# A two-layer encoder kernel: convolution sums moved into PSUM, fewer taps on GpSimd, softmax scaling on ScalarE

## The chip, the cores and the metric

The kernel runs on one core of one Trainium2 chip. The metric is the device time of one execution in microseconds (us), as the median of several runs. In the rows, PE is TensorE's matmuls and PEld its weight loads, DVE is VectorE, ACT is ScalarE, POOL is GpSimd, SP is SyncE. A row that begins with ACTq is ScalarE's instruction queue while it issues a DMA.

## What is computed

Two layers of an encoder run over two sequences of 256 tokens, with 1024 features. Layer 0 mixes with neighbourhood attention and a spatial gate; layer 1, the "second mixer", with latent attention beside a gated convolution of 31 taps. Each layer then has a feed-forward block. All arithmetic is in fp32, and matmuls with weights run on values split into a high and a low part. The change touches these parts of layer 1 (and, by a flag, the helper that both attentions share):

```python
def odd_mixer(x, ...):                      # the second mixer
    h = x @ w_in                            # c_q, c_kv, k_r, glu_a, glu_g
    c = latent_attention(c_q, c_kv, k_r, ...)         # rms norms, 8 heads, softmax
    d = glu_a * jax.nn.sigmoid(glu_g)                 # 512 channels
    d = jax.nn.silu(layernorm(dwconv(d, conv_w, conv_b), conv_ln_g, conv_ln_b))
    return jnp.concatenate([c, d], axis=-1) @ w_out
...
        p = jax.nn.softmax(s, axis=-1).astype(v.dtype)
        return jnp.einsum('bhqk,bkhd->bqhd', p, v_r)
```

`dwconv` is a depthwise convolution: each of the 512 channels is summed over 31 shifted copies of itself, each with its own weight.

## The kernel before

The program is one stream of work written in Python. A scheduler orders each engine's queue from it before the kernel runs; on the chip each engine works its queue strictly in order and waits on semaphores. Pools of tiles decide further waits: PSUM has eight banks of 128x512 fp32, four in pool `pA`, two in `pB`, two in `pC`.

The second mixer goes like this. `glu(i)` makes a quarter of the convolution's input, 128 channels by two sequences of 256 tokens: two groups of 24 matmuls, a sigmoid on ScalarE (`sig`), and a product on VectorE into `dpad[i]`, which has 15 zeros on both sides of each sequence. `cproj()` makes the inputs of the latent attention, and `chain()` norms them: ScalarE copies them from PSUM to `craw` and sums their squares, VectorE and GpSimd make the scale (`v`), VectorE applies it (`craw`, line 585), TensorE transposes. `kvproj()` and `qproj()` make keys, values and queries; the queries' rotary parts go into place by DMAs that ScalarE issues (line 623). `attend(p)` runs for four pairs of heads, each over two sequences, so 16 times in all for one head: scores (`s`) by TensorE into `pB`, the row maximum (`nmx`) on VectorE, the exponential (`er`) with row sums on ScalarE, the reciprocal (`ri`) and the scaling of the rows by it on VectorE (lines 484 to 487), a transpose (`pt`) on TensorE, a copy (`PTr`) on ScalarE, and the product with the values (`pv`).

The convolution has no need of TensorE. For each of the four quarters, VectorE makes the first tap and the bias (line 530) and adds one shifted, weighted copy after the other into `acc` in SBUF (line 680). The last `NPOOL` taps go another way: ScalarE multiplies the shifted input by its weight into a ring of two halves called `pr` (line 684; the first of them, line 532, goes straight into `acc2`), and GpSimd adds it to `acc2` (line 685). Line 686 adds the two sums. The scheduler spreads these instructions over VectorE's, ScalarE's and GpSimd's queues between those of the norms and the attention. After them come a layer norm over the channels (`conv_ln`: transposes `ct` and `cb`), the output projection (`op` and `dn`) and the feed-forward block.

Of the kernel before, what the change touches and what calls it, by code (L numbers as in the profile page):

```python
# [11 lines left out]
AF = mybir.ActivationFunctionType  # L12
# [10 lines left out]
LN_EPS = 1e-5  # L23
RMS_EPS = 1e-6
NPAIR = 22
NPOOL = 13
NWARM = 18
ACUT = 832
KEEP = {4: 0, 7: 1, 10: 2, 13: 3}
# [21 lines left out]
def tile_encoder(ctx: ExitStack, tc: tile.TileContext, I, O):  # L51
    nc = tc.nc
# [411 lines left out]

    pend = []

    def attention(p, score, V, mix, post, er, PTr):
        for s in range(2):
            PT = [PTr.get(), PTr.get()]
            pss = [bank(pB, "s").rearrange("p (a k) -> p a k", a=2) for _ in range(2)]  # L470
            for qt in range(2):
                for h in range(2):
                    score(pss[h][:, qt, :], h, slice(s * S + qt * P, s * S + qt * P + P), slice(s * S, s * S + S))
            for h in range(2):
                e = er.get()
                sc = post(pss[h], h, e)
                nmx = small(2, "nmx")
                nc.vector.tensor_reduce(out=nmx, in_=sc, axis=AX.X, op=ALU.max, negate=True)
                rs = small(2, "rs")
                for qt in range(2):  # L480
                    nc.scalar.activation(out=e[:, qt, :], in_=sc[:, qt, :], func=AF.Exp,  # L481
                                         bias=nmx[:, qt:qt + 1], accum_out=rs[:, qt:qt + 1])
                ri = small(2, "ri")
                nc.vector.reciprocal(out=ri, in_=rs)
                for qt in range(2):
                    nc.vector.tensor_scalar(out=e[:, qt, :], in0=e[:, qt, :], scalar1=ri[:, qt:qt + 1], scalar2=None,  # L486
                                            op0=ALU.mult)
                pt = bank(pC, "pt")
                for kc in range(2):
                    for qt in range(2):  # L490
                        nc.tensor.transpose(pt[:, (2 * kc + qt) * P:(2 * kc + qt + 1) * P],  # L491
                                            e[:, qt, kc * P:(kc + 1) * P], ident)
                nc.scalar.copy(out=PT[h], in_=pt.rearrange("p (k q) -> p k q", k=2))

            def pv_stage(s=s, PT=PT):
                pv = bank(pC, "pv")
                for kc in range(2):
                    for h in range(2):
                        mm(pv[h * 64:(h + 1) * 64, :S], V[s][:, kc, (2 * p + h) * 64:(2 * p + h + 1) * 64],
                           PT[h][:, kc, :], kc == 0, kc == 1)  # L500
                split(mix, pv[:, :S], slice(s * S, s * S + S))
            flush_pv()
            pend.append(pv_stage)
# [9 lines left out]

    def odd_mixer(xT):
        dpad = [None] * 4

        def glu(i, by_seq=False):
            pss = []
            for hi, lo in kept.pop(i, None) or glu_load(i):
                pss.append((bank(pA, "glu"), hi, lo))  # L520
            for seqs in ((0,), (1,)) if by_seq else ((0, 1),):
                for ps, hi, lo in pss:
                    gemm_feat(ps, hi, lo, xT, seqs)
            sg = tmp([P, 512], s="sig")
            nc.scalar.activation(out=sg, in_=pss[1][0], func=AF.Sigmoid)
            d = dpad[i]
            nc.vector.tensor_tensor(out=d[:, :, 15:15 + S], in0=pss[0][0].rearrange("p (s t) -> p s t", s=2),
                                    in1=sg.rearrange("p (s t) -> p s t", s=2), op=ALU.mult)
            a, a2 = acc[i // 2][:, i % 2], acc2[i // 2][:, i % 2]
            nc.vector.tensor_scalar(out=a, in0=d[:, :, 0:S], scalar1=pc("cw", i * 32),  # L530
                                    scalar2=pc("cw", i * 32 + 31), op0=ALU.mult, op1=ALU.add)
            nc.scalar.activation(out=a2, in_=d[:, :, 31 - NPOOL:31 - NPOOL + S], func=AF.Copy,
                                 scale=pc("cw", i * 32 + 31 - NPOOL))

# [116 lines left out]
        def attend(p):  # L651
            if p == 0:
                G["ring"] = Ring(2, "er"), Ring(2, "PTr")
            er, PTr = G["ring"]
            qT, kT = G["qT"], G["kT"]
            mixT[p] = act([P, 2, T], F32R, "mixT")
            if p == 2:
                G["sink"] = ToFeat(xscr[1], 1, last_mm[0], "ln1_g1", "ln1_b1", xscr[2], EARLY)
            attention(p, lambda out, h, qs, ks: mm(out, qT[p][0:96, h, qs], kT[p][0:96, h, ks], True, True),
                      G["V"], mixT[p], lambda ps, h, e: ps, er, PTr)  # L660

        mixT = [None] * 8
        glu(0, True)
# [11 lines left out]
        op = OutProj("wout1", mixT, [0, 1, 2, 3], [4, 5, 6, 7])  # L675
        op.first(0, (0, 1))
        for i in range(4):
            a, a2 = acc[i // 2][:, i % 2], acc2[i // 2][:, i % 2]
            for j in range(1, 31 - NPOOL):
                nc.vector.scalar_tensor_tensor(out=a, in0=dpad[i][:, :, j:j + S], scalar=pc("cw", i * 32 + j), in1=a,  # L680
                                               op0=ALU.mult, op1=ALU.add)
            for j in range(32 - NPOOL, 31):
                pr = pr_ring.get()
                nc.scalar.activation(out=pr, in_=dpad[i][:, :, j:j + S], func=AF.Copy, scale=pc("cw", i * 32 + j))  # L684
                nc.gpsimd.tensor_tensor(out=a2, in0=a2, in1=pr, op=ALU.add)  # L685
            nc.vector.tensor_tensor(out=a, in0=a, in1=a2, op=ALU.add)

        def conv_ln():
            for c in range(4):
# [191 lines left out]
```

## Time and profile before

| | before |
|---|---|
| time, median of 3 runs | 1159.08 us (1159.08 to 1159.62) |
| profiled execution, span | 1159.0 us |
| mean granted TensorE clock | 0.978 of full speed |
| busy share of the span | PE 96%, DVE 61%, ACT 42%, POOL 22% |

The profiled execution's span agrees with the median of the runs within 0.1 us, so a sum made against the span can be read as a time. In the profile, a line that gives 40 digits shows the busy share of 40 equal slices (29 us each) in tenths.

### The profile page before, as it was taken

How to read it: one execution, taken by the hardware profiler on the slowest of the kernel's cores; microseconds unless marked ns; L12 is line 12 of the kernel's file. 1: busy time of each engine (PE TensorE's matmuls, PEld its weight loads, DVE VectorE, ACT ScalarE, POOL GpSimd, SP SyncE). 2: the span in 40 equal slices, each digit the busy share in tenths (PEclk: the TensorE clock that was granted, in tenths of full speed). 3: DMA queues.
4: the chain of work that ended last, by engine and by line, in shares of the span. 5: the costliest groups of instructions: out<-in, count | busy, mean ns of one | idle time of the engine just before them, and what ended most of it. 6: DMA issues, size and time to landing. Idle time of an engine off the chain costs nothing.

```text
span 1159.0 us, 13693 instructions
## 1 busy us (share of the span) xinstructions
PE 1107.0 (96%) x5210; PEld 908.1 (78%) x5210; DVE 702.3 (61%) x1016; ACT 486.3 (42%) x765; POOL 259.1 (22%) x243
## 2 busy tenths in 40 slices
PE   9999999999999999999998658899999999999996
PEld 7787777988888888888887535689888888888884
DVE  3567774775565566323678999657755665642226
ACT  3534552644444444311555467346444444432110
POOL 4091011300000000007376656702000000000174
PEclk9999999999999999999998878999999999999998
DMA  8742104333223224553221121134332232223501
GB/s 254 238 118 73 55 20 171 133 115 108 91 93 108 91 92 140 186 198 100 106 81 49 28 73 43 67 109 140 116 106 95 91 104 97 91 99 101 199 38 73
DMA packets 36194, 124.34 MB, mean 107 GB/s; under 512 B 4352, under 2 KB 5120, under 8 KB 36128
## 3 DMA queue, kind: packets, MB, share of 16 engines
q1 hardware_dynamic: 28224, 99.10, 26.7%
q0 software_dynamic: 6480, 22.66, 5.4%
q10 hardware_dynamic: 1424, 1.71, 0.6%
q8 instruction: 41, 0.67, 0.2%
q14 instruction: 25, 0.20, 0.1%
HBM read 114.01 MB, written 8.39 MB: 106 GB/s over the span
## 4 chain that ended last, share of the span: by engine, by line
PE 83%; DVE 11%; DMA 2%; ACT 1%; issue 1%; POOL 1%; SPq 0%; POOLq 0%; ACTq 0%; DVEq 0%
PE up L96 42%; PE dn L96 25%; DVE acc L680 5%; PE qk L96 4%; PE op L96 4%; DMA raw<-in_wug 2%; PE s L96 2%; PE v L96 2%; DVE er L486 2%; PE pv L96 1%; DVE wlo L109 1%; PE glu L96 1%; PE lnT L233 1%; PE pt L491 1%; PE u L96 1%
## 5 line engine op out<-in xcount | busy, mean ns | idle before, releaser
L96 PE MATMUL up<-xT,whi 128*128 128x512 f32 (+1 forms) x1536 | 440.7, 372 | 0.4 <-DVE xT L245 0.4
L109 DVE TENSOR_TENSOR wlo<-raw,whi 128x1024 fp32r<-128x1024 f32 (+1 forms) x174 | 225.2, 1295 | 303.6 <-ACT whi L107 299.9
L96 PEld LDWEIGHTS up<-xT,whi 128*128 128x128 f32 x1536 | 280.1, 188 | 50.3 <-DVE xT L245 0.6
L107 ACT CAST whi<-raw 128x1024 fp32r<-128x1024 f32 (+1 forms) x174 | 182.5, 1050 | 262.4 <-PE dn L96 126.1
L96 PE MATMUL up<-xT,wlo 128*128 128x512 f32 (+1 forms) x768 | 283.8, 372 | 0.0
L96 PE MATMUL dn<-whi,gT 128*128 128x512 f32 x704 | 217.7, 390 | 0.0
L96 PEld LDWEIGHTS up<-xT,wlo 128*128 128x128 f32 x768 | 144.4, 188 | 25.1
L96 PEld LDWEIGHTS dn<-whi,gT 128*128 128x128 f32 x704 | 132.1, 188 | 27.2
L96 PE MATMUL dn<-wlo,gT 128*128 128x512 f32 x352 | 137.0, 389 | 0.0
L182 POOL DMA_DIRECT2D xres<-xscr x12 | 6.4, 540 | 574.4 <-PE dn L96 573.5
L685 POOL TENSOR_TENSOR acc<-acc,pr 128x512 f32<-128x512 f32 x48 | 77.3, 1610 | 46.4 <-ACT pr L684 44.2
L680 DVE SCALAR_TENSOR_TENSOR acc<-dpad,par,acc 128x512 f32<-128x512 f32 x68 | 78.3, 1177 | 0.5
L96 PEld LDWEIGHTS dn<-wlo,gT 128*128 128x128 f32 x352 | 66.1, 188 | 13.6
L113 ACT CAST gT<-cv 128x512 fp32r<-128x512 f32 x44 | 27.3, 620 | 112.2 <-DVE cv L742 112.2
L731 ACT ACTIVATE cv<-up,par 128x512 f32<-128x512 f32 x88 | 67.9, 772 | 0.0
L734 DVE SCALAR_TENSOR_TENSOR cv<-up,par,cv 128x510 f32<-128x510 f32 x88 | 65.8, 747 | 2.7
L732 DVE SCALAR_TENSOR_TENSOR cv<-up,par,cv 128x510 f32<-128x510 f32 x88 | 65.4, 743 | 0.0
L741 ACT ACTIVATE cv<-cv 128x512 f32<-128x512 f32 x44 | 27.8, 632 | 80.6 <-DVE cv L734 80.6
L114 DVE TENSOR_TENSOR gT<-cv,gT 128x512 fp32r<-128x512 f32 x44 | 30.4, 692 | 27.5 <-ACT gT L113 27.5
L96 PE MATMUL glu<-xT,khi 128*128 128x512 f32 (+1 forms) x160 | 44.0, 362 | 0.0
L96 PE MATMUL op<-whi,mixT 128*128 128x512 f32 x128 | 43.5, 398 | 0.0
L96 PE MATMUL dn<-whi,mixT 128*128 128x512 f32 x128 | 42.6, 395 | 0.7 <-ACT er L481 0.7
(193 smaller groups left out, 1397.8 us busy)
## 6 DMA issues: line engine op xcount, KB each, us to landing
raw<-in_wup SPq DMA_DIRECT2D x88, 512.0 KB, 3.4
raw<-in_wdn SPq DMA_DIRECT2D x44, 512.0 KB, 3.5
raw<-in_wout SPq DMA_DIRECT2D x16, 512.0 KB, 3.7
xscr<-xres POOLq DMA_DIRECT2D x12, 512.0 KB, 3.4
xres<-xscr POOLq DMA_DIRECT2D x12, 512.0 KB, 4.5
raw<-in_wqk SPq DMA_DIRECT2D x8, 512.0 KB, 4.6
raw<-in_wglu SPq DMA_DIRECT2D x8, 512.0 KB, 4.0
raw<-in_wug SPq DMA_DIRECT2D x7, 512.0 KB, 6.6
```

What stands on the lines that cost most here:

```text
L96: last_mm[0] = nc.tensor.matmul(out=out, lhsT=lhsT, rhs=rhs, start=first, stop=last)
L107: nc.scalar.copy(out=hi[:, :n], in_=raw[:, :n])
L109: nc.vector.tensor_tensor(out=lo[:, :n], in0=raw[:, :n], in1=hi[:, :n].bitcast(F32), op=ALU.subtract)
L113: nc.scalar.copy(out=dst[:, 0, sl], in_=src)
L114: nc.vector.tensor_tensor(out=dst[:, 1, sl], in0=src, in1=dst[:, 0, sl].bitcast(F32), op=ALU.subtract)
L486: nc.vector.tensor_scalar(out=e[:, qt, :], in0=e[:, qt, :], scalar1=ri[:, qt:qt + 1], scalar2=None, op0=ALU.mult)
L680: nc.vector.scalar_tensor_tensor(out=a, in0=dpad[i][:, :, j:j + S], scalar=pc("cw", i * 32 + j), in1=a, op0=ALU.mult, op1=ALU.add)
L685: nc.gpsimd.tensor_tensor(out=a2, in0=a2, in1=pr, op=ALU.add)
L731: nc.scalar.activation(out=c, in_=pv, func=AF.Identity, scale=pc(fw, ch * 4 + 1), bias=pc(fw, ch * 4 + 3))
L732: nc.vector.scalar_tensor_tensor(out=c[:, :, 1:S], in0=pv[:, :, 0:S - 1], scalar=pc(fw, ch * 4), in1=c[:, :, 1:S], op0=ALU.mult, op1=ALU.add)
L734: nc.vector.scalar_tensor_tensor(out=c[:, :, 0:S - 1], in0=pv[:, :, 1:S], scalar=pc(fw, ch * 4 + 2), in1=c[:, :, 0:S - 1], op0=ALU.mult, o ...
L741: nc.scalar.activation(out=cg, in_=cg, func=AF.Silu)
```

## The change

`NPOOL` goes from 13 to 10, so that for each quarter VectorE has 20 additions instead of 17 and ScalarE and GpSimd 9 instead of 12. VectorE's running sum lives in a PSUM bank of its own for each quarter (`accps[i]`, from `pA`) instead of in SBUF; the last addition of the quarter reads that bank and `acc2` and writes `acc`. The last `glu` takes its two banks from `pB` instead of `pA`. In the second mixer's attention, ScalarE scales the softmax rows; in the first layer's, VectorE still does.

```diff
-NPOOL = 13
+NPOOL = 10
...
-    def attention(p, score, V, mix, post, er, PTr):
+    def attention(p, score, V, mix, post, er, PTr, on_act=False):
...
                 for qt in range(2):
-                    nc.vector.tensor_scalar(out=e[:, qt, :], in0=e[:, qt, :], scalar1=ri[:, qt:qt + 1], scalar2=None,
-                                            op0=ALU.mult)
+                    if on_act:
+                        nc.scalar.activation(out=e[:, qt, :], in_=e[:, qt, :], func=AF.Copy, scale=ri[:, qt:qt + 1])
+                    else:
+                        nc.vector.tensor_scalar(out=e[:, qt, :], in0=e[:, qt, :], scalar1=ri[:, qt:qt + 1],
+                                                scalar2=None, op0=ALU.mult)
...
         dpad = [None] * 4
+        accps = [None] * 4
...
-                pss.append((bank(pA, "glu"), hi, lo))
+                pss.append((bank(pB if i == 3 else pA, "glu"), hi, lo))
...
-            a, a2 = acc[i // 2][:, i % 2], acc2[i // 2][:, i % 2]
+            accps[i] = bank(pA, "cacc")
+            a, a2 = accps[i].rearrange("p (s t) -> p s t", s=2), acc2[i // 2][:, i % 2]
             nc.vector.tensor_scalar(out=a, in0=d[:, :, 0:S], scalar1=pc("cw", i * 32),
                                     scalar2=pc("cw", i * 32 + 31), op0=ALU.mult, op1=ALU.add)
...
-                      G["V"], mixT[p], lambda ps, h, e: ps, er, PTr)
+                      G["V"], mixT[p], lambda ps, h, e: ps, er, PTr, True)
...
-            a, a2 = acc[i // 2][:, i % 2], acc2[i // 2][:, i % 2]
+            a, a2 = accps[i].rearrange("p (s t) -> p s t", s=2), acc2[i // 2][:, i % 2]
             for j in range(1, 31 - NPOOL):
                 nc.vector.scalar_tensor_tensor(out=a, in0=dpad[i][:, :, j:j + S], scalar=pc("cw", i * 32 + j), in1=a,
                                                op0=ALU.mult, op1=ALU.add)
...
-            nc.vector.tensor_tensor(out=a, in0=a, in1=a2, op=ALU.add)
+            nc.vector.tensor_tensor(out=acc[i // 2][:, i % 2], in0=a, in1=a2, op=ALU.add)
```

The scheduler makes new queues from this. Three places show how. A row gives the line, the operation, out<-in, the tile's size, and how many such instructions stand in a row.

First, ScalarE's queue in the norms of `chain()`, just before the copies (`craw`) of the second sequence. Before:

```order
L684 ACTIVATE pr_4430<-dpad_4410,par 128x512 x2
L107 CAST whi_5490<-raw_5488 128x1024
L684 ACTIVATE pr_4430<-dpad_4410,par 128x512
L107 CAST whi_5794<-raw_5792 128x1024
L684 ACTIVATE pr_4430<-dpad_4410,par 128x512 x4
L559 COPY craw_4662<-dn_718_4539 128x416
L559 COPY craw_4662<-dn_719_4540 128x416
```

The same place in the changed program:

```order
L689 ACTIVATE pr_4430<-dpad_4410,par 128x512 x2
L107 CAST whi_5494<-raw_5492 128x1024
L689 ACTIVATE pr_4430<-dpad_4410,par 128x512
L107 CAST whi_5786<-raw_5784 128x1024
L689 ACTIVATE pr_4430<-dpad_4410,par 128x512
L564 COPY craw_4663<-dn_719_4540 128x416
L564 COPY craw_4663<-dn_720_4541 128x416
```

All of a quarter's `pr` products still stand ahead of the copies, but they are three fewer.

Second, VectorE's queue in the first heads of the attention (`acc_4423` and `cacc_5110` are the running sum of the last quarter). Before:

```order
L484 RECIPROCAL ri_5180<-rs_5177 128x2
L478 TENSOR_REDUCE nmx_5204<-s_5198 128x2
L680 SCALAR_TENSOR_TENSOR acc_4423<-dpad_4419,par,acc_4423 128x512
L486 TENSOR_SCALAR er_5110<-er_5110,ri_5180 128x256 x2
L680 SCALAR_TENSOR_TENSOR acc_4423<-dpad_4419,par,acc_4423 128x512
L484 RECIPROCAL ri_5209<-rs_5206 128x2
L478 TENSOR_REDUCE nmx_5219<-s_5199 128x2
```

In the changed program:

```order
L478 TENSOR_REDUCE nmx_5164<-s_5158 128x2
L685 SCALAR_TENSOR_TENSOR cacc_5110<-dpad_4419,par,cacc_5110 128x512 x3
L484 RECIPROCAL ri_5169<-rs_5166 128x2
L478 TENSOR_REDUCE nmx_5179<-s_5159 128x2
L685 SCALAR_TENSOR_TENSOR cacc_5110<-dpad_4419,par,cacc_5110 128x512 x4
L484 RECIPROCAL ri_5184<-rs_5181 128x2
L478 TENSOR_REDUCE nmx_5208<-s_5202 128x2
```

The scalings have left this queue, and up to four additions in a row now stand ahead of a head's reciprocal.

Third, ScalarE's queue in the same heads. Before:

```order
L684 ACTIVATE pr_4430<-dpad_4419,par 128x512
L481 ACTIVATE er_5109,rs_5206<-s_5198,nmx_5204 128x256 x2
L684 ACTIVATE pr_4430<-dpad_4419,par 128x512
L493 COPY PTr_5114<-pt_5169 128x512
L684 ACTIVATE pr_4430<-dpad_4419,par 128x512
L481 ACTIVATE er_5109,rs_5221<-s_5199,nmx_5219 128x256 x2
```

In the changed program:

```order
L481 ACTIVATE er_5114,rs_5181<-s_5159,nmx_5179 128x256 x2
L689 ACTIVATE pr_4430<-dpad_4419,par 128x512
L496 COPY PTr_5118<-pt_5173 128x512
L487 ACTIVATE er_5114<-er_5114,ri_5184 128x256 x2
L481 ACTIVATE er_5113,rs_5210<-s_5202,nmx_5208 128x256 x2
L487 ACTIVATE er_5113<-er_5113,ri_5213 128x256 x2
```

The two scalings of a head stand behind its exponentials in ScalarE's queue, in places directly behind them, and wait for the reciprocal that VectorE makes in between.

## Rows read from the trace of the kernel before

**Rows 1.** The page: busy shares, then VectorE and TensorE's clock in 40 slices.

```profile
PE 1107.0 (96%) x5210; PEld 908.1 (78%) x5210; DVE 702.3 (61%) x1016; ACT 486.3 (42%) x765; POOL 259.1 (22%) x243
...
DVE  3567774775565566323678999657755665642226
...
PEclk9999999999999999999998878999999999999998
```

**Rows 2.** Chain that ended last, 590.6 to 742.8 us, shares by engine and line.

```profile
by line: DVE acc L680 41.8%; DVE er L486 12.7%; issue 5.9%; DVE wlo L109 5.3%; POOL acc L685 4.0%; DVE nmx L478 3.5%; PE s L96 3.0%; PE pv L96 2.4%; PE pt L491 2.3%; DVE acc L530 1.6%; DVE qr L618 1.6%; DVE craw L585 1.1%; POOL v L584 1.1%;
```

**Rows 3.** Busy time by stretch: length, then each engine (instructions), granted clock, DMA.

```profile
590.60:624.70 34.10, 28.43 (x132) 24.09 (x130) 33.50 (x55) 17.23 (x37) 27.20 (x20) 0.93 0.21 62
624.70:681.60 56.90, 41.57 (x169) 33.28 (x167) 53.65 (x58) 34.06 (x54) 31.36 (x21) 0.89 0.13 33
681.60:742.80 61.20, 46.38 (x222) 32.27 (x224) 59.80 (x103) 37.51 (x106) 42.39 (x33) 0.81 0.19 69
742.80:785.50 42.70, 42.70 (x206) 34.42 (x207) 20.39 (x39) 18.55 (x28) 9.62 (x8) 0.96 0.27 88
```

**Rows 4.** Groups of VectorE, one window for each of the first three stretches.

```profile
L680 DVE SCALAR_TENSOR_TENSOR acc<-dpad,par,acc 128x512 f32<-128x512 f32 x17 | 19.4, 1140 | 0.3
...
L680 DVE SCALAR_TENSOR_TENSOR acc<-dpad,par,acc 128x512 f32<-128x512 f32 x36 | 42.8, 1235 | 0.1
...
L486 DVE TENSOR_SCALAR er<-er,ri 128x256 f32<-128x256 f32 x32 | 24.3, 795 | 0.0
L680 DVE SCALAR_TENSOR_TENSOR acc<-dpad,par,acc 128x512 f32<-128x512 f32 x16 | 17.9, 1121 | 0.0
```

**Rows 5.** Lines 680, 530 and 734: minimum, median and maximum of one, in ns.

```profile
L680 DVE SCALAR_TENSOR_TENSOR acc<-dpad,par,acc x68: 733/752/1796, 591.2 to 712.1; 128x512 f32<-128x512 f32 x68
...
L530 DVE TENSOR_SCALAR acc<-dpad,par x4: 533/545/1508, 590.7 to 675.0; 128x512 f32<-128x512 f32 x4
...
L734 DVE SCALAR_TENSOR_TENSOR cv<-up,par,cv x88: 735/748/750, 229.0 to 1030.7; 128x510 f32<-128x510 f32 x88
```

**Rows 6.** Timeline of VectorE, then GpSimd: start, us, what; `glu` and `q` are PSUM.

```profile
663.08 1.40 DVE L680 SCALAR_TENSOR_TENSOR acc<-dpad,par,acc 128x512 f32<-128x512 f32 x2
...
671.19 1.56 DVE L680 SCALAR_TENSOR_TENSOR acc<-dpad,par,acc 128x512 f32<-128x512 f32 x1
672.67 0.68 DVE L527 TENSOR_TENSOR dpad<-glu,sig 128x512 f32<-128x512 f32 x1
673.27 1.18 DVE L621 TENSOR_TENSOR qr<-qr,qr 128x512 f32<-128x512 f32 x1
...
670.93 2.97 POOL L685 TENSOR_TENSOR acc<-acc,pr 128x512 f32<-128x512 f32 x2 [10.25 <-ACT pr L684]
```

**Rows 7.** VectorE's groups by length, 800 to 1000 us: 1024 and 512 elements.

```profile
L109 DVE TENSOR_TENSOR wlo<-raw,whi 128x1024 fp32r<-128x1024 f32 x38 | 46.5, 1224 | 60.1 <-ACT whi L107 60.1
...
L742 DVE TENSOR_TENSOR cv<-cv,cv 128x512 f32<-128x512 f32 x19 | 13.1, 691 | 0.6
```

**Rows 8.** Groups of ScalarE, 590.6 to 742.8 us.

```profile
L684 ACT ACTIVATE pr<-dpad,par 128x512 f32<-128x512 f32 x48 | 33.8, 721 | 14.8 <-POOL acc L685 14.8
L481 ACT ACTIVATE er<-s,nmx 128x256 f32<-128x256 f32 x32 | 14.9, 472 | 15.2 <-DVE nmx L478 13.6 <-DVE mv L159 1.6
L493 ACT COPY PTr<-pt 128x512 f32<-128x512 f32 x16 | 9.1, 586 | 6.7 <-PE pt L491 6.7
...
L113 ACT CAST mixT<-pv 128x256 fp32r<-128x256 f32 x6 | 2.3, 376 | 1.7 <-PE pv L96 1.7
```

**Rows 9.** GpSimd's additions (minimum, median, maximum) and its residual rows (mean), in ns.

```profile
L685 POOL TENSOR_TENSOR acc<-acc,pr x48: 1260/1604/2342, 592.1 to 717.3; 128x512 f32<-128x512 f32 x48
...
L190 POOL TENSOR_TENSOR xres<-xres,rowg 128x1024 f32<-128x1024 f32 x4 | 9.6, 2416 | 4.6 <-DMA rowg<-in_rows 4.6
```

**Rows 10.** Timeline of ScalarE's queue ahead of the first exponential.

```profile
667.03 2.50 ACTq L623 DMA_DIRECT2D qT<-qr  x4
669.58 0.60 ACT L525 ACTIVATE sig<-glu 128x512 f32<-128x512 f32 x1 [10.30 <-DMA qT<-qr]
670.07 1.32 ACT L684 ACTIVATE pr<-dpad,par 128x512 f32<-128x512 f32 x2
...
674.49 2.45 ACTq L623 DMA_DIRECT2D qT<-qr  x4
```

## The prediction

> **What bounds the kernel now.** The page comes first: TensorE is busy for 96% of the span, but around slices 20 to 25 VectorE's digits reach 9 while the granted clock falls to 0.7 and 0.8 [rows 1]. The chain of waits over that piece, 590.6 to 742.8 us, then says who ends it: the convolution's additions 41.8%, the scaling of softmax rows 12.7% [rows 2]. The table by stretch shows where [rows 3]. I cut it at three events: stretch A ends when ScalarE takes the first normed transposes (624.7), B with the first exponential (681.6), C with ScalarE's last `PTr` copy (742.8). VectorE is busy for 33.5 of 34.1, 53.65 of 56.9 and 59.8 of 61.2 us. TensorE's busy time times its clock is 28.43 x 0.93 + 41.57 x 0.89 + 46.38 x 0.81 = 101 us, so its work at full clock would leave 51 of the 152 us free. Stretch D, to 785.5, is 42.7 us of 42.7 on TensorE: the change adds no matmul there, and nothing in it can shrink.
>
> **Why an addition is dear.** The 68 additions take 752 ns in the middle but up to 1796 [rows 5]; their means by stretch are 1140, 1235 and 1121 [rows 4]. The long ones meet GpSimd. While GpSimd adds from 670.93 to 673.90, VectorE's instructions with two SBUF inputs take 1.56 and 1.18 us, but line 527 between them, with one input in PSUM and one in SBUF, takes 0.68 [rows 6]. The changed addition has one input in SBUF and one in PSUM too, so I expect it never to wait. Its own price: line 734 has the same operation with a PSUM source and 510 elements at 748 ns [rows 5]. Back to back, two free additions occupy 1.40 us where two of 0.74 stand, so 0.08 overlaps [rows 6]: 0.67 us each. No row writes to PSUM from VectorE. From below I take 0.67; from above a second pass over the 512 elements, which rows of 1024 and 512 elements price at 1.22 - 0.69 = 0.53 us [rows 7], so 1.20. A gain from writing there has no row; the lower end already is a free addition. I take 0.70, near the row that shares the operation and a PSUM operand.
>
> The Trainium skill (VectorE: DVE Perf Modes, The TRN2 errata) speaks against this: it gives an instruction with PSUM source 62 cycles more fixed cost than one from SBUF, an estimate of 65 ns. The rows show 748 against a minimum of 733 [rows 5], so the trace does not agree with that size. By the page the 17 additions that gate stretch A would each take 0.05 more and the time would be 0.8 us higher than my sum.
>
> **Stretch A, the norms.** VectorE's queue gates it. Ahead of the last normed row stand 17 additions before and 17 now; the three extra ones come behind. Before they took 17 x (1.14 - 0.08) = 18.0 us [rows 4], now 17 x 0.70 = 11.9: 6.1 less. GpSimd has 9 additions instead of 12 and is no longer held by VectorE, so the other instructions that meet it (weights' low parts, norms) should lose some waits, 1.5 us chosen out of 0 to 3. Against this, VectorE now comes earlier to the first squares than ScalarE makes them, 1.1 us. ScalarE's copies of the second sequence, behind three fewer products, are ready before VectorE asks for them. **A: -6.5 us** (-3 to -9).
>
> **Stretch B, keys, queries, two quarters of the convolution.** VectorE: 53.65 less 42.8 - 36 x 0.08 = 39.9 [rows 4], plus 40 additions x 0.70 = 28, plus two low parts of weights that come over from C, 2.4: 44 us. TensorE: 41.57 x 0.89 = 37 plus some 3 for two matmul groups that come over. Neither is the longest now. ScalarE is: 34.1 busy [rows 3], 2.2 for a cast and two copies from C, three groups of four DMAs that it issues at about 2.5 us a group [rows 10], and nine products in a row for one quarter, paced by GpSimd: 1260 ns at best, say 1.35 in a row [rows 9], against 0.63 for a product (0.72 less its overlap, two taking 1.32 [rows 8, 10]), so 9 x 0.72 = 6.5. That is 50.3. What ScalarE still waits for the other engines I put at 2.7; before, it idled for 22.8, of which 10.3 for queries whose rotary half VectorE made late [rows 10]. The sum is 53. **B: -3.9 us** (-7 to +1).
>
> **Stretch C, sixteen heads.** VectorE: 59.8 less the scalings, 24.3 - 32 x 0.08 = 21.7, less 16 additions, 17.9 - 1.3 = 16.6 [rows 4], less 2.4 moved to B, plus 19 x 0.70 = 13.3: 32.4 us. ScalarE: 37.5 [rows 3] less nine products at 0.63 (16 before, 7 now), less the 2.2 moved to B, plus 32 scalings. No row has a scaling of 256 elements with a column of scales on ScalarE. The product of 512 takes 721; 256 elements fewer are worth 586 - 376 = 210 [rows 8]; so 0.51, and 0.42 with the overlap of 0.09. Below lies the plain cast at 0.376, above the exponential with its bias column at 0.472 plus the same overlap, 0.56; ends 0.29 and 0.47 in a row. 32 x 0.42 = 13.4, and ScalarE has 37.5 - 5.7 - 2.2 + 13.4 = 43.0 us. TensorE's 46.38 x 0.81 = 37.6 fits below. So ScalarE becomes the bound of C, and its queue brings a new wait: behind each pair of exponentials stands its scaling, which waits for a reciprocal that VectorE makes behind up to four additions, and behind the scaling wait the next exponential and a `PTr` copy. With a copy or product between in most heads I put this at 0.3 us a head, 4.8 in all. C takes 47.8. GpSimd's later work (residual rows, whose instructions take 2.4 us each [rows 9]) moves forward with the heads and meets no scaling. **C: -13.4 us** (-19 to -3).
>
> The Trainium skill (ScalarE: Activation LUTs, What ACT_TABLE_LOAD costs) has the price that no row has: an estimate of 186 + 0.833 x 256 + 93 = 492 ns for such a scaling, 93 of it overlapped. By it C would be 0.6 us shorter than by my sum.
>
> **Sum.** The smaller edits cost nothing that shows. The first tap of a quarter (line 530) goes from 545 ns [rows 5] to about the price of an addition, some 0.2 us four times: in B and C VectorE's slack covers three of them, uncovered they cost 0.2 each. The last `glu` waits for `pB` banks that the queries leave: TensorE's 7 us of slack in B cover it. Both attentions share the helper, but the first mixer's scaling stays as it is. 1159.1 - 6.5 - 3.9 - 13.4 = **1135.3 us**.
>
> **Rivals.**
> *ScalarE's waits take most of it back.* If a head costs 1.0 us of waiting rather than 0.3, C is 11 us longer: 1146.5. For it: three or four additions ahead of a reciprocal are 2.1 to 2.8 us, longer than the exponentials; ScalarE now both makes and consumes in one queue. Against: only some five heads have so many, and later heads have none.
> *Every wait falls away.* C runs at ScalarE's 43 and B at 50: 1127.8, and if GpSimd's pace is better still, about 1122. TensorE's cap is 1159 - 51 = 1108. Against: half the stretch would still be a chain from engine to engine, and TensorE's clock in C was 0.81 with engines waiting so [rows 3].
> *The sum in PSUM waits for GpSimd all the same,* so that the edit does not do what it says: 80 additions at 1.10 to 1.15. A loses its gain (+0.7), B is VectorE's 53.65 - 39.9 + 46 + 2.4 = 62 (+5.5), C stays ScalarE's (-13.4): 1152. Line 527's 0.68 speaks against it.
> *Slower: reading and writing one PSUM bank costs a second pass,* 1.20 an addition. A +2.4; B 53.65 - 39.9 + 48 + 2.4 = 64.2 (+7.3); in C four additions hold a reciprocal for 4.8 us, so ScalarE gives back about 6 of its 13.4 (-7.4): 1161.4. It decides from about 1.16 us an addition upward. Nothing in the trace excludes it; each addition already reads what the one ahead of it wrote.
>
> **How the numbers follow.** The forecast's own case, 1128 to 1142, has 0.52; all waits gone 0.15; ScalarE's waits 0.20; waits on GpSimd all the same 0.06; a second pass 0.07, of which 0.02 lands within 0.2% (2.3 us, about what a measurement of this kernel tells from no change) and 0.05 beyond it. That gives faster 0.93 less 0.02 for mishaps in the third case: 0.91, same 0.04, slower 0.05. The range from 1121 to 1151 leaves out the last two cases and the far end of the second.
>
> **What would show it.** After the change, additions between 0.73 and 0.80 us with no long ones would prove the price; a median above 1.1 the fourth rival; a spread up to 1.7 the third. The first transposes should reach ScalarE near 618, the first exponential near 671, the last `PTr` copy near 719, and the stretch behind it should still be about 42.7 us of full TensorE. ScalarE should be the busiest engine of C at some 43 us, and what ends its idle time should be VectorE's reciprocal. I would be wrong if a new wait sits elsewhere: a `glu` group held by a PSUM bank that a running sum still occupies, or ScalarE's nine products in a row keeping a sigmoid from VectorE.

## The result and the profile after

| | before | after |
|---|---|---|
| time, median (4 runs each) | 1159.35 us (1159.08 to 1160.47) | 1129.67 us (1128.52 to 1130.66) |
| ratio to before | | 0.974, 95% interval 0.9727 to 0.9753 |
| profiled execution, span | 1159.0 us | 1128.1 us |
| mean granted TensorE clock | 0.978 | 0.988 |

The change made the kernel 29.7 us faster; 23.8 were forecast. One run of an experiment below, the first of e1's four, took 1389.83 us with TensorE's clock at 0.75 of full speed, and no number here uses it. The page of the changed kernel answers to [rows 1]:

```profile
PE 1100.6 (98%) x5210; PEld 903.9 (80%) x5210; DVE 664.6 (59%) x996; ACT 491.0 (44%) x785; POOL 231.6 (21%) x231
...
PE   9999999999999999999998989999999999999995
...
DVE  3567773686656565432369987567656566552226
...
PEclk9999999999999999999999989999999999999998
```

TensorE's row of the kernel before, which [rows 1] do not have:

```profile
PE   9999999999999999999998658899999999999996
```

In the middle of the span TensorE shows two 8s where it had 8, 6, 5, 8, 8, and the clock one 8 where it had 8, 8, 7, 8. The table by stretch, cut at the same events as [rows 3], says where the time came from:

```profile
core 0: us, PE busy (x) PEld busy (x) DVE busy (x) ACT busy (x) POOL busy (x), PEclk, DMA share, GB/s
588.85:615.25 26.40, 24.49 (x121) 20.81 (x119) 25.71 (x53) 14.86 (x34) 19.13 (x17) 1.00 0.28 81
615.25:665.96 50.71, 44.05 (x178) 34.25 (x177) 48.07 (x73) 36.65 (x58) 25.96 (x21) 0.93 0.21 57
665.96:712.10 46.14, 43.59 (x223) 31.61 (x223) 33.17 (x73) 41.49 (x124) 24.95 (x23) 0.85 0.20 69
712.10:754.66 42.56, 41.21 (x203) 33.51 (x204) 23.59 (x40) 19.14 (x31) 13.10 (x10) 1.00 0.27 87
```

A went from 34.1 to 26.4 us, B from 56.9 to 50.7, C from 61.2 to 46.1, and D stayed (42.7 and 42.6): 29.1 us in all. Another 1.75 us lie ahead of A, in program text that is the same. The point where A begins wandered between 586.8 and 589.9 us over the profiles of this study, and variants of the changed kernel are found near both ends (586.8 in e9, 589.8 in e8), so I do not count these 1.75 us as the change's. From here on kernels are compared by the stretches between the first `dpad` product and the first `up` matmul, 195.4 us before and 166.4 after; what follows takes 373.6 to 375.1 us in every one. (A begins a little earlier by this rule than in the table above: 27.2 us for 26.4.)

VectorE's additions by stretch (A, B, C) answer to [rows 4]. One that crosses a boundary is counted on both sides, so the counts come to 82 for 80. Below them are the fewest, median and most nanoseconds of an addition, of GpSimd's addition and of ScalarE's scaling, which answer to [rows 5, 9] or had no row:

```profile
L685 DVE SCALAR_TENSOR_TENSOR cacc<-dpad,par,cacc 128x512 f32<-128x512 f32 x17 | 12.7, 749 | 0.2
...
L685 DVE SCALAR_TENSOR_TENSOR cacc<-dpad,par,cacc 128x512 f32<-128x512 f32 x46 | 33.7, 751 | 1.4 <-DVE cacc L685 0.7
...
L685 DVE SCALAR_TENSOR_TENSOR cacc<-dpad,par,cacc 128x512 f32<-128x512 f32 x19 | 14.3, 752 | 0.4
```

```profile
L685 DVE SCALAR_TENSOR_TENSOR cacc<-dpad,par,cacc x80: 739/753/760, 589.7 to 684.7; 128x512 f32<-128x512 f32 x80
...
L690 POOL TENSOR_TENSOR acc<-acc,pr x36: 1265/1292/2328, 590.4 to 677.5; 128x512 f32<-128x512 f32 x36
...
L487 ACT ACTIVATE er<-er,ri x32: 492/518/553, 667.5 to 708.6; 128x256 f32<-128x256 f32 x32
```

No addition is longer than 760 ns, although GpSimd adds beside them for 50 us. Before, the longest took 1796 and the mean was 1121 to 1235.

### The profile page after: what moved, and what is told of

Same layout as the page of the kernel before. It is cut to its first block, busy times and chain, and to the rows that moved or that the text cites. A ratio compares the mean times of both kernels' runs of the same rounds, so it can differ in the third digit from the quotient of the medians.

```text
span 1128.1 us, 13661 instructions
## 1 busy us (share of the span) xinstructions
PE 1100.6 (98%) x5210; PEld 903.9 (80%) x5210; DVE 664.6 (59%) x996; ACT 491.0 (44%) x785; POOL 231.6 (21%) x231
## 5 line engine op out<-in xcount | busy, mean ns | idle before, releaser
L685 DVE SCALAR_TENSOR_TENSOR cacc<-dpad,par,cacc 128x512 f32<-128x512 f32 x80 | 59.2, 751 | 2.0 <-DVE cacc L685 0.7
L690 POOL TENSOR_TENSOR acc<-acc,pr 128x512 f32<-128x512 f32 x36 | 49.7, 1381 | 35.6 <-ACT pr L689 33.9
L96 PE MATMUL op<-whi,mixT 128*128 128x512 f32 x128 | 43.6, 399 | 0.0
```

Source lines behind the costliest of these rows:

```text
L96: last_mm[0] = nc.tensor.matmul(out=out, lhsT=lhsT, rhs=rhs, start=first, stop=last)
```

## The experiments

All of them in one table; `sum` is A to D, and C and D stand together because in some kernels TensorE does part of D's work before ScalarE's last `PTr` copy, the event that divides them. The times are medians, the ratios go against runs of the kernel before made beside each experiment (medians of 1159.5 to 1161.1 us), and the stretches are those of one profiled execution. In e3 that execution was 3.3 us above the median, in e10 2.1 above, in e11 1.4 below; in the others it lies within 0.8 us.

| kernel | sums in | taps GpSimd | scaling on | time, us | ratio to before | A | B | C+D | sum |
|---|---|---|---|---|---|---|---|---|---|
| before | SBUF | 13 | VectorE | 1159.35 | | 34.8 | 56.9 | 103.7 | 195.4 |
| after | PSUM | 10 | ScalarE | 1129.67 | 0.9740 | 27.2 | 50.8 | 88.5 | 166.4 |
| e1 | SBUF | 10 | ScalarE | 1150.58, 1150.52 | 0.9919 (0.9890 to 0.9948) | 31.8 | 58.9 | 96.4 | 187.1 |
| e2 | PSUM | 10 | VectorE | 1137.15 | 0.9799 (0.9775 to 0.9824) | 27.0 | 50.4 | 95.7 | 173.1 |
| e3 | PSUM | 13 | ScalarE | 1133.56 | 0.9774 (0.9746 to 0.9801) | 29.3 | 50.5 | 91.9 | 171.7 |
| e4 | PSUM | 13 | VectorE | 1139.97 | 0.9838 (0.9819 to 0.9857) | 29.5 | 51.5 | 94.2 | 175.1 |
| e5 | SBUF | 13 | ScalarE | 1155.36 | 0.9965 (0.9952 to 0.9978) | 34.6 | 56.9 | 99.3 | 190.8 |
| e6 | SBUF | 10, not added | ScalarE | 1121.95 | one run | 25.5 | 42.3 | 91.3 | 159.0 |
| e7 | PSUM | 10 | ScalarE | 1127.47 | 0.9719 (0.9691 to 0.9748) | 27.1 | 48.0 | 89.0 | 164.1 |
| e8 | PSUM | 10 | none | 1127.81 | one run | 27.2 | 50.3 | 84.9 | 162.4 |
| e9 | PSUM | 8 | ScalarE | 1130.54 | 0.9748 (0.9734 to 0.9763) | 26.7 | 53.0 | 88.4 | 168.1 |
| e10 | PSUM | 10 | ScalarE | 1126.42 | 0.9716 (0.9702 to 0.9731) | 24.1 | 49.9 | 89.3 | 163.3 |
| e11 | PSUM | 10 | ScalarE | 1129.31 | 0.9741 (0.9725 to 0.9757) | 24.2 | 44.6 | 96.0 | 164.8 |

### e1: the sums back in SBUF

```diff
-            accps[i] = bank(pA, "cacc")
-            a, a2 = accps[i].rearrange("p (s t) -> p s t", s=2), acc2[i // 2][:, i % 2]
+            a, a2 = acc[i // 2][:, i % 2], acc2[i // 2][:, i % 2]
```

> The changed kernel with one part undone: the running sums of the 20 additions per group lie in SBUF again; 10 taps on GpSimd and the scaling on ScalarE stay. Theory 1 (an addition whose running sum is in SBUF stands still while GpSimd adds, one in PSUM doesn't): the 80 additions have a tail again, mean 0.95 to 1.1 us instead of 0.75, which is 16 to 28 us more on VectorE; stretches A and B get back most of what they lost, C a part, and the time is about 1145 us (1139 to 1152). Rival 2 (where the sum lies hardly matters; the gain is that GpSimd has fewer additions and VectorE no scaling): additions near 0.80, time 1129 to 1133 us.

The trace by stretches comes from a second run:

> The changed kernel with the running sums in SBUF once more, for its trace by stretches (the first one's profiled execution had TensorE at a lowered clock from start to end). Theory 1: additions of 1.05 to 1.1 us in the mean with a tail up to 1.8 us; A some 8 us longer than in the changed kernel, B some 8, C some 5. Rival 2: the additions cost the same and the 22 us lie in TensorE's waits in C alone.

Time 1150.58 and 1150.52 us, at the far end of the first theory's range. The additions, fewest, median and most nanoseconds:

```profile
L683 DVE SCALAR_TENSOR_TENSOR acc<-dpad,par,acc x80: 733/752/1801, 589.2 to 708.0; 128x512 f32<-128x512 f32 x80
```

The median is that of PSUM (752 against 753 ns); the tail up to 1801 is back, and with it a total of 84.8 us for 80 additions, 25.6 more than in PSUM. The stretches A, B and C with D lose 4.6, 8.1 and 7.9 us, 20.7 in all (8, 8 and 5 had been expected for A, B and C): the second theory falls.

### e6: is it GpSimd, or SBUF itself?

The edit goes against e1; GpSimd's additions are left out:

```diff
                 nc.scalar.activation(out=pr, in_=dpad[i][:, :, j:j + S], func=AF.Copy, scale=pc("cw", i * 32 + j))
-                nc.gpsimd.tensor_tensor(out=a2, in0=a2, in1=pr, op=ALU.add)
```

> The changed kernel with the running sums in SBUF, and GpSimd's 36 additions left out (so nine of the 31 taps' products of each group are computed and never added). Theory 1 (what lengthens an addition in SBUF is GpSimd adding beside it): the 80 additions take 0.73 to 0.76 us each with no tail, and A to C are as short as with sums in PSUM or shorter, 1124 to 1130 us. Rival 2 (reading and writing the running sum in SBUF is itself slow): their mean stays at 1.0 us or above, time near 1150 us.

Again the fewest, median and most nanoseconds of an addition, and then two groups of the norms in A (mean ns of one behind the comma):

```profile
L683 DVE SCALAR_TENSOR_TENSOR acc<-dpad,par,acc x80: 741/747/755, 588.9 to 680.2; 128x512 f32<-128x512 f32 x80
```

```profile
L588 DVE TENSOR_SCALAR craw<-craw,v 128x256 f32<-128x256 f32 x4 | 1.4, 348 | 0.1
...
L572 DVE TENSOR_TENSOR craw<-ra,rb 128x32 f32<-128x32 f32 x4 | 0.7, 182 | 0.0
```

With GpSimd silent 80 additions in SBUF take 741 to 755 ns, the same as in PSUM beside a busy GpSimd. So the cause is shown from both sides: take away GpSimd or take the running sum out of SBUF, and the tail goes. The time of 1121.95 us says that GpSimd's company still costs the changed kernel something; the norms in A show where. Line 588 (590 in the changed kernel) and line 572 (574) take 348 and 182 ns here, and 625 and 694 there:

```profile
L574 DVE TENSOR_TENSOR craw<-ra,rb 128x32 f32<-128x32 f32 x4 | 2.8, 694 | 0.0
L590 DVE TENSOR_SCALAR craw<-craw,v 128x256 f32<-128x256 f32 x4 | 2.5, 625 | 0.0
```

### e2, e3, e4 and e5: each part without the others

```diff
-                      G["V"], mixT[p], lambda ps, h, e: ps, er, PTr, True)
+                      G["V"], mixT[p], lambda ps, h, e: ps, er, PTr)
```

This is e2, against the changed kernel. e3 has `NPOOL = 13` in it, e4 both (so that only the sums' place differs from before), e5 `NPOOL = 13` and e1's edit (so that only the scaling differs from before).

> The changed kernel with one part undone: VectorE scales the softmax rows again, sums in PSUM and 10 taps on GpSimd stay. VectorE then has 32 more instructions in C. Theory 1 (they were 0.80 us in the mean because they stood still beside GpSimd's additions, too): GpSimd adds in only a part of C, so they cost 0.4 to 0.8 us, 13 to 25 us on an engine that is busy for 33 of C's 46 us; C becomes 4 to 10 us longer, time 1137 us (1133 to 1141). Rival 2 (C is now set by TensorE and its lowered clock, not by VectorE or ScalarE): ScalarE's relief and VectorE's load both lie beside it, time 1128 to 1132 us.

> The changed kernel with one part undone: GpSimd adds 13 taps per group again, so 17 additions per group on VectorE (12 fewer in all, some 9 us) and 12 more products on ScalarE (8.7 us) and additions on GpSimd (16.6 us). Theory 1 (B is paced by the products that wait for GpSimd, 1.37 us apiece): B is 3 to 5 us longer, A a little shorter, time 1133 us (1130 to 1137). Rival 2 (VectorE still sets A and B): 6 to 8 us faster, 1122 to 1124 us. Rival 3 (TensorE sets all of it): within 1 us of 1129.7.

> The kernel before with one part of the change alone: the running sums in PSUM; 13 taps on GpSimd and the scaling on VectorE stay. Undone from the changed kernel, the sums' place cost 22 us, the scaling 7 to 8 and the taps 4. Theory 1 (the three parts relieve different engines at different places and nearly add up): 1159.4 less 18 to 22 us, 1139 us (1136 to 1143). Rival 2 (the parts need each other: with 13 taps the products pace B and with the scaling VectorE stays the longest in C): gain of 8 to 13 us, 1146 to 1151 us.

> The kernel before with one part of the change alone: ScalarE scales the softmax rows; sums in SBUF and 13 taps on GpSimd stay. Theory 1 (the scaling is worth what undoing it cost, since C's second half has no additions left and VectorE is then relieved of 64 instructions): 5 to 9 us faster than before, 1152 us (1150 to 1155). Rival 2 (the additions of group 3, which stand still beside GpSimd, go on into C and set its end, so ScalarE's relief comes too late): within 3 us of before, 1156 to 1160 us. Rival 3 (the forecast of C, in which VectorE's scaling set it all): 11 to 13 us faster, 1146 to 1148 us.

e2 came at 1137.15 and e3 at 1133.56, both where their first theories had them for the time. e3's reason was wrong, though: B did not grow (50.5 against 50.8), and the loss is 2.2 us in A and 3.4 in C and D. Its second theory, that VectorE sets A and B, falls for B as well: VectorE's busy time there went from 48.1 to 42.5 us, and B stayed as long. e4 gave 1139.97, its first theory. e5 gave 1155.36, a gain of 4.3 us over the runs beside it (1159.64), just short of its first theory's 5 to 9 and far from the 11 to 13 of the forecast's view of C. (The scalings are 32 instructions, as e2's expectation and the rows have it, not the 64 that those of e5 and e8 give.)

Put in one after another, the sums in PSUM bring 20.3 us of the stretches (195.4 to 175.1, e4), the scaling 3.4 more (171.7, e3), the three fewer taps 5.4 more (166.4). By the median times the same three steps are 19.4, 6.4 and 3.9 us (e3's profiled execution was the slowest of its four). In the other order the scaling brings 4.7 (e5), the taps 3.7 (e1) and the sums 20.7, by the times 4.0, 4.8 and 20.9. The parts add up in either order to within some 3 us, and the sums are two thirds to seven tenths of the gain. They are most of C's, too: with them alone C and D fall by 9.5 us, with the scaling alone by 4.4.

What the scaling costs on VectorE is told by its groups in e2: in the first mixer (where GpSimd adds nothing), in C's first half and in its second, mean nanoseconds of one behind the comma, and then for all 64 the fewest, median and most:

```profile
L489 DVE TENSOR_SCALAR er<-er,ri 128x256 f32<-128x256 f32 x32 | 10.5, 371 | 0.1
...
L489 DVE TENSOR_SCALAR er<-er,ri 128x256 f32<-128x256 f32 x14 | 7.3, 560 | 0.0
...
L489 DVE TENSOR_SCALAR er<-er,ri 128x256 f32<-128x256 f32 x18 | 15.2, 887 | 0.0
```

```profile
L489 DVE TENSOR_SCALAR er<-er,ri x64: 321/348/2478, 102.6 to 717.3; 128x256 f32<-128x256 f32 x64
```

371 ns become 560 in the half with the convolution's additions on GpSimd and 887 in the half with its residual rows, though a scaling has only one input tensor. The 887 is again a mean over waiting: four of the 18, which start with GpSimd's residual rows at 702 and 709 us, take 4.76 and 4.87 us a pair; of the other seven pairs six take 0.58 to 0.68.

### e8: what sets C now?

```diff
-                    if on_act:
-                        nc.scalar.activation(out=e[:, qt, :], in_=e[:, qt, :], func=AF.Copy, scale=ri[:, qt:qt + 1])
-                    else:
+                    if not on_act:
```

> The changed kernel with the scaling of the second mixer's softmax rows left out on every engine (so its rows are not divided by their sums). It takes 64 instructions, some 29 us back to back, from ScalarE, nearly all of them in C. Theory 1 (ScalarE sets C, as forecast): C falls from 46 to 38 us or less, time 1119 to 1122 us. Rival 2 (TensorE sets C: 37 us of work at full clock, part of it at half clock): C falls by 2 to 4 us only, time 1125 to 1128 us. Rival 3 (C is set ahead of the heads' end by the convolution's norms): no change, 1129 to 1130 us.

C fell by 3.7 us for 11.5 us less of work on ScalarE (29.95 busy against 41.49; the 29 us of the expectation were too many): the second theory. The one run's time, 1127.81 us, is in that theory's range too. The stretches of the changed kernel, and then of e8, in the columns shown first, cut where TensorE's clock returns:

```profile
666.00:682.00 16.00, 13.55 (x43) 8.83 (x44) 14.21 (x27) 15.39 (x44) 9.62 (x8) 0.57 0.01 2
682.00:712.00 30.00, 30.00 (x182) 22.77 (x180) 18.81 (x47) 25.96 (x81) 15.19 (x15) 1.00 0.30 106
```

```profile
667.30:684.00 16.70, 15.69 (x62) 10.44 (x64) 12.97 (x26) 13.23 (x38) 9.68 (x8) 0.69 0.01 1
684.00:709.70 25.70, 25.37 (x158) 18.93 (x155) 19.25 (x47) 16.72 (x55) 14.33 (x14) 1.00 0.34 123
```

In the changed kernel C is two stages. For 16 us ScalarE is full (15.39 of 16.00), and TensorE, at a mean clock of 0.57, is idle for 2.45 us, all in waits for ScalarE's exponentials, and works mostly at half speed. The 30 us behind them are TensorE's, busy for all of them at full clock, with ScalarE at 25.96. Without the scaling the first stage is no shorter (16.70), but TensorE does 15.69 x 0.69 = 10.8 us of full-speed work in it instead of 13.55 x 0.57 = 7.7. These 3.1 us are most of the 4.3 by which the second stage is shorter.

### e9: the other side of the number of taps

The edit is `NPOOL = 8`.

> The changed kernel with 8 taps per group on GpSimd instead of 10, so 22 additions per group on VectorE (8 more in all, 5.5 us back to back) and 8 fewer products on ScalarE and additions on GpSimd. Theory 1 (VectorE, busy for 48 of B's 51 us, sets A and B): some 4 to 5 of the 8 fall ahead of the first exponential, 2 to 5 us slower, 1132 to 1135 us. Rival 2 (the products that GpSimd paces set B, as forecast, with 7 waits of 0.64 us apiece): 2 to 4 us faster, 1126 to 1128 us.

1130.54 us, between the two theories' ranges. B grew by 2.2 us and the sum by 1.7: the direction of the first theory, less than its size. The time's interval overlaps that of the changed kernel, so between 8 and 10 taps the timing decides nothing. B's growth shows as waits of TensorE: ahead of the last `glu`'s end they come to 6.0 us (2.37 for a sigmoid, 2.55 for a copy of the values, 1.06 for a query's rotary part), against 3.5 in the changed kernel.

### e7, e10 and e11: what can still be had

e7 gives the third `glu` group the other pool, `pB if i >= 2 else pA`.

> The changed kernel, with the third glu group's two products in the pool of two banks instead of the pool in which the running sums lie. In the changed kernel that group's first product waits 2.65 us for the bank of the first running sum, with TensorE idle, and the granted clock is 0.54 to 0.61 for the 8 us behind it, which costs some 3.4 us. Theory 1 (the bank is what it waits for, and the idle time is what the low clock follows): both go, 5 to 6 us faster, 1124 us (1123 to 1127). Rival 2 (the group then waits for the compressed rows' banks in the same small pool, and the projections behind it for the group's own two banks): the wait only moves, 1128 to 1133 us.

TensorE's row around that group, in the changed kernel and then in e7:

```profile
615.68 0.33 PE L594 MATMUL dn<-ident,craw 128*128 128x128 f32 x1 [0.41 <-DVE craw L590]
618.65 1.22 PE L96 MATMUL glu<-xT,khi 128*128 128x512 f32 x2 [2.65 <-DVE acc L691]
```

```profile
614.55 0.48 PE L594 MATMUL dn<-ident,craw 128*128 128x128 f32 x1 [0.42 <-DVE craw L590]
614.86 1.22 PE L96 MATMUL glu<-xT,khi 128*128 128x512 f32 x2
```

The wait of 2.65 us for line 691, VectorE's last addition of the first quarter, is gone: it was the bank. The clock still falls behind the norms' idle bits (0.68 in 616 to 619), and B is 2.8 us shorter, half of what was expected. The sum is 2.2 us lower; the time, 1127.47 us, is just short of the first theory's range, and the interval of the time overlaps that of the changed kernel.

e10 is e7 with group 0's GpSimd additions held back until the norms' last transpose (`G["ctr"]`; `after_mm` makes an instruction wait for a matmul):

```diff
-                nc.gpsimd.tensor_tensor(out=a2, in0=a2, in1=pr, op=ALU.add)
+                ga = nc.gpsimd.tensor_tensor(out=a2, in0=a2, in1=pr, op=ALU.add)
+                if i == 0:
+                    after_mm(ga, G["ctr"])
```

> The version with the third glu group in the other pool, and group 0's nine GpSimd additions held until the last transpose of the compressed rows, so that GpSimd does not add while the rows are normed. In the changed kernel VectorE's small instructions of the norms (line 590: 0.37 and 0.63 us, line 574: 0.69, line 569: 0.41) meet GpSimd; with GpSimd silent they took 0.28, 0.35, 0.18 and 0.19, some 4.4 us less in all. Theory 1 (they gate stretch A): A 3 to 4 us shorter, GpSimd's additions all find room behind it, time 1123 to 1125 us. Rival 2 (GpSimd then is late: its 36 additions take 50 us from 612 on, so the first two groups' sums end late and B grows): 1127 to 1131 us.

```profile
L590 DVE TENSOR_SCALAR craw<-craw,v 128x256 f32<-128x256 f32 x4 | 1.4, 340 | 0.0
...
L574 DVE TENSOR_TENSOR craw<-ra,rb 128x32 f32<-128x32 f32 x4 | 0.7, 186 | 0.0
```

The norms' instructions are as short as with GpSimd silent, and A is 3.0 us shorter than in e7 with TensorE never idle. But B is 1.9 longer and C and D 0.3: A's gain is mostly given back, since GpSimd's 36 additions now all lie behind it (ScalarE's last products before the first exponential wait 0.66 and 1.04 us for them). At 1126.42 us this is the fastest version tried that leaves no work out, about 3 us below the changed kernel; the two intervals touch (0.9702 to 0.9731, 0.9727 to 0.9753).

e11 is e10 ("the run beside it") with `glu(3)` written behind the first pair of heads and its banks in `pA`.

> As the run beside it, and the fourth glu group written behind the first pair of heads, with its products in the larger pool: two of the query projections then stand between the first score products in TensorE's row. Theory 1 (the lowered clock of C's first 15 us, 0.50, follows TensorE's idle 3 us ahead of it, and work put there keeps it up): 3 to 6 us faster than the run beside it, 1118 to 1121 us. Rival 2 (the first heads are a chain through VectorE and ScalarE with too little TensorE work in any case): the clock falls all the same, within 1.5 us of the run beside it.

TensorE's wait for the first exponential in the changed kernel and in e11, and e11's clock behind it (the columns of the stretches as above):

```profile
667.03 1.62 PE L96 MATMUL s<-kT,qT 96*128 96x256 f32 x4 [3.05 <-ACT er L481]
```

```profile
657.39 2.08 PE L96 MATMUL s<-kT,qT 96*128 96x256 f32 x4 [4.47 <-ACT er L481]
```

```profile
656.00:660.00 4.00, 2.11 (x5) 1.22 (x5) 2.79 (x6) 3.99 (x10) 1.83 (x2) 0.55 0.00 0
...
672.00:676.00 4.00, 4.00 (x15) 2.46 (x16) 3.89 (x7) 4.00 (x13) 3.13 (x3) 0.50 0.00 0
...
700.00:704.00 4.00, 1.64 (x8) 0.94 (x7) 0.75 (x2) 3.96 (x7) 4.00 (x3) 1.00 0.00 0
704.00:708.00 4.00, 3.73 (x17) 2.12 (x18) 0.14 (x2) 3.95 (x10) 4.00 (x3) 0.57 0.00 0
```

For the clock the second theory holds: TensorE waits 4.47 us instead of 3.05 (3.38 in e10), the clock falls to 0.50 all the same and stays there to 676, and behind a second idle piece (1.64 busy of 4.00 at 700) it falls again. The time is outside both theories: 2.9 us above e10, where the second allowed 1.5. Whether the clock would stay up if the first heads never left TensorE idle was not reached by any of these kernels and stays open.

## Why the prediction was right

**The price of an addition.** 0.70 us an addition was taken, 0.67 to 1.20 the ends: measured are 749 to 752 ns apiece and, by stretch, 12.7 / 17 = 0.75, 33.7 / 46 = 0.73 and 14.3 / 19 = 0.75 us of VectorE's busy time. That GpSimd would not hold it is shown by the spread (739 to 760) and, from both sides, by e1 and e6. Third and fourth rival are out. The size of 0.67 for additions in a row was read from a pair that goes into two different sums [rows 6]; into the same sum it is 0.79 (shown at the end), and of the 48 additions that directly follow another 38 are of that kind. In A the 17 took 0.8 us more than forecast.

The Trainium skill (VectorE: DVE Perf Modes, The TRN2 errata) would, by an estimate from its 62 cycles, have PSUM sources some 65 ns dearer; a median of 747 in SBUF beside a silent GpSimd (e6) against 753 in PSUM does not bear this out for this operation. The forecast's 0.05 an addition and 0.8 us do not follow from that estimate: 65 ns on top of 0.67 are 0.035 above the 0.70 taken, 0.6 us in A.

**A.** -6.5 forecast, -7.7 measured. The 17 additions went from 19.4 (17 x 1.14, [rows 4]) to 12.7 us, 6.7 less (6.1 forecast); the waits for ScalarE's squares that I had put at 1.1 came to 0.4. The other instructions of VectorE were to lose 1.5 us of waits; they lost 1.1, but some 1.0 of it are two instructions that now lie behind the end of A. The rest kept its waits for GpSimd, as the norms' lines under e6 show.

**B.** -3.9 forecast, -6.2 measured, and here a step failed: "Neither is the longest now. ScalarE is". VectorE is fuller, busy for 48.1 of 50.7 us, and ScalarE for 36.7. The forecast had counted 17, 40 and 19 additions in A, B and C, 76 of the 80; B has 45, with one more that ends in C. ScalarE's waits in B (engine, tile and line that waits, what for, us in all, times, longest):

```profile
ACT pr L689 <- POOL acc L690: 6.2, 8, 1.2
ACT qT L633 <- PE q L96: 2.8, 2, 2.1
ACT sig L529 <- PE glu L96: 2.4, 2, 2.3
ACT kT L654 <- issue: 1.4, 1, 1.4
ACT acc L537 <- DVE dpad L531: 0.8, 1, 0.8
```

The products' waits for GpSimd cost 6.2 us against 6.5 forecast. The mistake is the three groups of DMAs at 2.5 us: ScalarE's queue issues them while copies and products run, and of 7.5 us only 1.4 appear as empty time. The waits for TensorE and VectorE erred the other way, 6.0 us for 2.7. So the sum of 53 came near the measured 50.7 because two errors nearly cancelled.

Nor does VectorE alone set B, full as it is: e3 takes 5.7 us of its work out of B, and B stays; e7 takes none from it but removes a wait of TensorE, and B is 2.8 us shorter. In the changed kernel it is TensorE's row that is nearly without gaps, in the columns of the stretches, from the end of its wait for the bank to the end of the last `glu`:

```profile
618.65:661.30 42.65, 41.71 (x168) 32.68 (x168) 40.33 (x61) 29.47 (x47) 24.19 (x19) 0.95 0.21 56
```

It is busy for all but 0.9 of these 42.65 us. Ahead of them it waited 2.65 us for the bank, and behind them a chain of sigmoid, scores, maximum and exponential ends B. Its work in B, 44.05 x 0.93 = 41 us, had been forecast well (40); that B would end with it had not.

**C.** -13.4 forecast, -15.1 measured. The loads were sized well (ScalarE 41.5 for 43.0, VectorE 33.2 for 32.4, TensorE 43.59 x 0.85 = 37.1 for 37.6; a scaling 0.518 us and 0.41 in a row, for 0.51 and 0.42), but "ScalarE becomes the bound of C" fits the first 16 us at most; e8 shows TensorE behind the other 30. ScalarE's waits for a reciprocal, put at 4.8 us, came to 1.1; 2.7 went to TensorE's transposes instead. Nor is ScalarE the busiest engine of C, as it should have been: TensorE is, for 43.6 us. So the sum 43.0 + 4.8 came near 46.1 by the wrong road, and the gain is less the scaling's than the additions': e4 shows that the sums' place took 10.0 of C's 15.1 us by itself. VectorE's load alone had not been the bound: e5, with the scalings on ScalarE and the sums still in SBUF, has VectorE busy in C for 40.13 us where it was 59.80 [rows 3], and C is only 3.1 us shorter. The stretch C of e4 and of e5:

```profile
669.10:720.30 51.20, 41.53 (x222) 29.75 (x224) 48.45 (x101) 31.84 (x97) 31.61 (x26) 0.92 0.17 62
```

```profile
680.20:738.30 58.10, 47.57 (x222) 31.99 (x224) 40.13 (x72) 49.23 (x138) 39.60 (x31) 0.79 0.20 73
```

In e5 the forecast's new wait does occur: ScalarE's scalings wait 6.1 us for reciprocals, which stand behind additions of 1126 ns in the mean. With additions of 752 ns it is the 1.1 us above.

The Trainium skill (ScalarE: Activation LUTs, What ACT_TABLE_LOAD costs) gives an estimate of 492 ns for such a scaling; the shortest of 32 took that, the median 518.

**D and the rest.** 0 forecast, -0.1 measured; the 1.75 us ahead of A are not the change's. The profiled span fell by 30.9 us where 23.8 were forecast: 1.2 of the difference are in A, 2.3 in B, 1.7 in C, 0.1 in D and 1.75 at the start.

**What I named as a way to be wrong** did occur: a `glu` group stood 2.65 us for a bank that a running sum occupied. It cost about 2 us (e7), covered by B's larger gain. The other one, products that keep a sigmoid from VectorE, did not.

## What to carry to other kernels

A mean of 1.14 us over a median of 0.75 is a mean over waiting: look at the fewest and the most of a group before pricing it, and ask which engine is active beside the long ones. An operand moved out of SBUF can be worth more than work moved to another engine: 20 of 29 us here, and in e4 VectorE has as many instructions as before (1016). When a sum of engine loads comes out near the measured stretch, cut the stretch in two and look at who is full in each half, since a relief of the engine that the sum named may bring a third of what it seems to.

## What was unexpected of the hardware

An instruction of VectorE need not have two input tensors in SBUF to stand still beside GpSimd: scalings with one input went from 371 to 887 ns in the mean, the longest to 2478 (e2). Nor need it be large: with two inputs of 128x32 elements the mean is 182 with GpSimd silent (e6) and 694 beside it (the changed kernel). An addition with one input in SBUF and the other in PSUM, with its result in PSUM, stood at 739 to 760 throughout. The Trainium skill (SBUF — State Buffer, Who interferes with whom) says so of both: instructions with two inputs in SBUF, and scalings and copies in a two-port mode, share ports with GpSimd, and one with at most one input in SBUF outside such a mode doesn't. The trace agrees on what waits and what doesn't; that these scalings run in such a mode no row here shows.

VectorE's additions in a row come in two paces. Both of these rows are from B of the changed kernel, 0.79 and 0.67 us apiece:

```profile
621.63 10.25 DVE L685 SCALAR_TENSOR_TENSOR cacc<-dpad,par,cacc 128x512 f32<-128x512 f32 x13
...
634.61 6.67 DVE L685 SCALAR_TENSOR_TENSOR cacc<-dpad,par,cacc 128x512 f32<-128x512 f32 x10
```

By the order of VectorE's queue, the thirteen all add to the second quarter's sum, and the ten alternate between the second's and the third's. The same holds throughout: where one addition directly follows another in the changed kernel, all ten that go into a different sum start 0.66 us after it, and 36 of 38 that go into the same sum 0.78 to 0.80 (the other two stand behind a gap). With sums in SBUF and GpSimd silent (e6) it is 0.66 for 25 and 0.78 to 0.79 for 20, so the place of the sum is not the reason. To alternate two quarters wherever one stands in a row would, as an estimate, free at most 38 x 0.13 = 5 us of VectorE's row; it was not tried.

GpSimd gained as well: the mean of its 48 additions fell from 1610 ns to 1375 when nothing but VectorE's sums left SBUF (e4); in the changed kernel it is 1381.

TensorE's clock fell to 0.50 of full speed, the lower of its levels (1.2 GHz), behind an idle piece of 3.05 us in the changed kernel and of 4.47 in e11, and stayed there while TensorE worked again: it was busy for 13.55 of the 16 us from 666 on. As an estimate from the mean clocks of its stretches, the changed kernel spends some 14 of C's 46 us at the lower level, e8 some 10 of 42 and e11 more than 20 of 61.
